# Attention, keys, values and gates: one more step between copies and the matmuls that read them, and matmuls of zeros at the start

## The chip, the core and the metric

The kernel runs on one core of a Trainium2 chip. The time is device microseconds of the whole program; three runs of the kernel before gave 1306.21, 1309.69 and 1312.1 us, median 1309.69. Names of engines: PE is TensorE (matmuls and transposes), DVE is VectorE, ACT is ScalarE, POOL is GpSimd, SP is SyncE, which issues the DMAs.

## The reference, cut to what matters

One layer of a hybrid decoder for 1024 prompt tokens and 32 sample tokens, in float32. An input projection of 22 column tiles feeds two groups of heads: four gated-delta heads (a chunked recurrence with a triangular inverse, decays from a gate) and eight heads of sliding-window attention with a learned sink. Then an output projection with a residual and a LayerNorm, a SwiGLU layer with a residual and a second LayerNorm. The parts that the change touches are the gate and the window attention:

```python
g = -jnp.exp(a_log) * jax.nn.softplus(a_a + dt_bias)        # gate: cumulated over a chunk
s = jnp.einsum('bnqhgd,bnkhd->bnhgqk', qb, kbk) * (HD_B ** -0.5)
s = jnp.where(mask, s, -jnp.inf)
p = jax.nn.softmax(jnp.concatenate([s, sink], axis=-1), axis=-1)[..., :KB]
o = jnp.einsum('bnhgqk,bnkhd->bnqhgd', p, vbk)
x = layernorm(ALPHA * x + m)                                 # ssum: the sum over D for the mean
```

## The kernel before, in words

All tokens are held with features on partitions. The tokens are cut in two halves, s = 0 (512 columns) and s = 1 (512 and the 32 sample columns, done as 272 + 272). Every float32 product is made of three matmuls on numbers split in a high and a low part (lines 426 to 428: high weight by high x, high weight by low x, low weight by high x). ACT writes the high part, DVE the low part (lines 161 and 162 for weights, 345 and 346 for x).

For each half `mix_in` runs through the projections one after the other (`dense`), and between two parts of a `dense` it calls `unit`, which lets the waiting pieces of attention, gates and recurrence take their next steps. Such a piece is a Python generator: it issues instructions, then yields the time that its PE work is worth; `pump` gives each generator one step at a call until a budget (2750, then 3000) is used up. A `yield 0.0` costs no budget, but what follows it is issued one `unit` later, so that more dense matmuls stand in front of it on PE. On top of that a scheduler places the issued instructions on each engine by its own estimate of the times, so the order on an engine is not that of the code alone. Each engine then runs its queue in order.

PSUM has eight banks: four for `dense` ("acc") and four for everything else ("ms"). SBUF pages come from pools ("hp", "xs", "xp"); taking a page issues a POOL memset of one column (line 228), which waits until the last user of that page is done. So POOL, too, has a queue in which a memset can stand in front of work.

The pieces that the change touches:
- `gating` (from line 480): transposes the gate inputs, a chain of some 25 short DVE and ACT operations, then matmuls at lines 537 to 541 that cumulate over time, a transpose at 555.
- `delta_k`: transposes at line 654 and products at 656 of the keys of the delta heads. `sample_attn`, `sample_delta`: the sample tokens; their updated states go out at line 1413 (`out_S_s`).
- `keys` and `vals`: split or transpose keys and values (lines 973, 995, 1002).
- `attn` (for each half four members m, each the heads m and m + 4, two members at a time): scores at lines 1059 and 1060, masking on DVE at 1063, exp on ACT at 1077, scaling on DVE at 1085; then for four tiles n the transposes at 1100, the copy from PSUM at 1104 (DVE for even n, ACT for odd n) and the product with the values at 1112.
- `out_proj` and `ln1`: DVE writes a residual tile `ac` (line 1681), POOL adds it up in `sum` (1683, 1685), PE takes the mean by a matmul with ones (1474).

Of the kernel before, what the change touches and what calls it, by code (L numbers as in the profile page):

```python
# [15 lines left out]
P = 128  # L16
# [77 lines left out]
NXP = 19  # L94
NRAW = 8
NSPLIT = 4
HLEAD = 5
HLAG = 3

# [108 lines left out]
def _program(k):  # L208
    nc, I, O = k.nc, k.I, k.O
    mm = nc.tensor.matmul  # L210
# [105 lines left out]
    def have(tag, n=1):  # L316
        while not room(tag, n):
            yield BLOCK
# [18 lines left out]
    def x_item(s, kt):  # L337
# [12 lines left out]

        return fin

    W.load(1)
    fins = [x_item(0, kt) for kt in range(3)]
    W.load(2)
# [128 lines left out]
    def gating(s, baT):  # L484
        w = 16 + s
        g = {}
        gt = small([P, 21, 17], "gt", 2)
        names = ["beta", "x", "ab", "y", "den", "y2", "pl", "gg", "gc", "gtot", "gd", "eg", "egl", "ekd", "bg", "ngc"]
        for i, n in enumerate(names):
            g[n] = gt[:, i, :]  # L490
        g["t"] = gt
        gba = gt[:, 16:18, :]
        pk = gt.rearrange("p a b -> p (a b)")[:, 18 * 17:18 * 17 + 32].rearrange("p (k w) -> p k w", w=16)
        gat[s] = g
        yield from have("ms")
        pt = bank()
        for n in range(4):
            tr(pt[:, n * 8:(n + 1) * 8], baT[:, n * P:(n + 1) * P], ident[:8, :8])
        if s:
            tr(pt[0:32, 32:40], baT[:, 512:544], ident[:8, :8])  # L500
        drop()
        V.tensor_copy(gba[:, :, 0:16].rearrange("p k (h n) -> p k h n", n=4),
                      pt[:, 0:32].rearrange("p (n k h) -> p k h n", k=2, h=4))
        if s:
            for h in range(4):
                V.tensor_copy(gba[32 * h:32 * h + 32, :, 16:17],
                              pt[0:32, 32:40].rearrange("p (k h) -> p k h", h=4)[:, :, h:h + 1])
        drop("ms")
        q = {n: g[n][:, :w] for n in names}
        A.activation(q["beta"], gba[:, 0, :w], AF.Exp, scale=-1.0)  # L510
        V.tensor_tensor(q["x"], gba[:, 1, :w], DT[:, :w], ALU.add)
        V.scalar_tensor_tensor(q["ab"], q["x"], -1.0, q["x"], ALU.mult, ALU.max)
        A.activation(q["y"], q["ab"], AF.Exp, scale=-1.0)
        yield 300.0
        V.tensor_scalar(q["beta"], q["beta"], 1.0, None, ALU.add)
        V.reciprocal(q["beta"], q["beta"])
        V.tensor_scalar(q["den"], q["y"], 2.0, None, ALU.add)
        V.reciprocal(q["den"], q["den"])
        V.tensor_tensor(q["y"], q["y"], q["den"], ALU.mult)
        V.tensor_tensor(q["y2"], q["y"], q["y"], ALU.mult)  # L520
        pl = q["pl"]
        V.tensor_scalar(pl, q["y2"], 1.0 / 13, 1.0 / 11, ALU.mult, ALU.add)
        for cf in (9, 7, 5, 3, 1):
            V.tensor_tensor(pl, pl, q["y2"], ALU.mult)
            V.tensor_scalar(pl, pl, 1.0 / cf, None, ALU.add)
        V.scalar_tensor_tensor(pl, pl, 2.0, q["y"], ALU.mult, ALU.mult)
        V.tensor_scalar(q["x"], q["x"], 0.0, None, ALU.max)
        V.tensor_tensor(pl, pl, q["x"], ALU.add)
        V.scalar_tensor_tensor(q["gg"], pl, -1.0, EA[:, :w], ALU.mult, ALU.mult)
        if s:  # L530
            yield from have("hp")
            su, so = late("SU", "SO")
        yield 0.0
        yield from have("ms")
        gg = g["gg"]
        pg = bank()
        mm(pg[:, 0:16], C["U"], gg[:, 0:16], start=True, stop=True)
        mm(pg[:, 17:33], C["ones"], gg[:, 0:16], start=True, stop=True)
        if s:
            mm(pg[:, 16:17], su, gg[:, 16:17], start=True, stop=True)  # L540
            mm(pg[:, 33:34], so, gg[:, 16:17], start=True, stop=True)
            drop()
        V.tensor_copy(gt[:, 8:10, :w], pg[:, 0:34].rearrange("p (k w) -> p k w", w=17)[:, :, :w])
        drop("ms")
        V.tensor_tensor(q["gd"], q["gtot"], q["gc"], ALU.subtract)
        A.activation(gt[:, 11:14, :w], gt[:, 8:11, :w], AF.Exp)
        V.tensor_tensor(q["bg"], q["beta"], q["eg"], ALU.mult)
        V.tensor_scalar(q["ngc"], q["gc"], -1.0, None, ALU.mult)
        V.tensor_copy(pk[:, 0, :], g["gc"][:, 0:16])
        V.tensor_copy(pk[:, 1, :], g["beta"][:, 0:16])  # L550
        yield 700.0
        yield from have("ms")
        yield from have("hp")
        pp = bank()
        tr(pp[:32, :P], pk.rearrange("p k w -> p (k w)"), ident)
        gT = page([32, P], F32, f"gT{s}")
        V.tensor_copy(gT, pp[:32, :P])
        drop("ms")
        gd = k.dp.tile([32, P], F32, name=f"gd{s}")
        dma(out=gd, in_=gT)  # L560
        drop()
        g["dram"] = gd
        flags.add(("g", s))
        yield 150.0
# [391 lines left out]
    def keys(s, kb):  # L956
        yield from have("hp", 4)
        kh = [page([P, 512], F32R, f"kh{s}{i}") for i in range(2)]
        kl = [page([P, 512], F32R, f"kl{s}{i}") for i in range(2)]
        for i in range(2):  # L960
            a, o = slice(64 * i, 64 * i + 64), slice(64 - 64 * i, 128 - 64 * i)
            A.copy(kh[i][a, :], kb[a, 0:512])
            A.copy(kh[i][o, :], kb[a, 0:512])
            V.tensor_tensor(kl[i][a, :], kb[a, 0:512], kh[i][a, :].bitcast(F32), ALU.subtract)
            V.tensor_tensor(kl[i][o, :], kb[a, 0:512], kh[i][a, :].bitcast(F32), ALU.subtract)
            yield 0.0
        at[s, "k"] = (kh, kl)
        if s:
            G.tensor_copy(ksT, kb[:, 512:544])
            yield from have("ms")  # L970
            yield from have("hp")
            pt = bank()
            tr(pt[:, 0:P], kb[:, 384:512], ident)
            tr(pt[0:32, P:2 * P], kb[:, 512:544], ident)
            kp = page([P, 2, P], F32, "kp")
            V.tensor_copy(kp[:, 0, :], pt[:, 0:P])
            V.tensor_copy(kp[0:32, 1, :], pt[0:32, P:2 * P])
            drop("ms")
            dma(out=O["k_p"], in_=kp[:, 0, :])
            dma(out=O["k_s"][:, 124:128, :], in_=kp[0:32, 1, :])  # L980
            drop()
            dma(out=O["k_s"][:, 0:124, :], in_=I["cache_k"][:, 4:128, :])
            dma(out=O["v_s"][:, 0:124, :], in_=I["cache_v"][:, 4:128, :])
        drop()
        flags.add(("keys", s))
        yield 300.0

    def vals(s, vT):
        yield from have("hp")
        vN = page([P, 4, P], F32, f"vN{s}")  # L990
        yield 0.0
        yield from have("ms")
        pv = bank()
        for n in range(4):
            tr(pv[:, n * P:(n + 1) * P], vT[:, n * P:(n + 1) * P], ident)
        V.tensor_copy(vN, pv.rearrange("p (n t) -> p n t", t=P))
        drop("ms")
        if s:
            dma(out=O["v_p"], in_=vN[:, 3, :])
            yield from have("ms")  # L1000
            pt = bank()
            tr(pt[0:32, 0:P], vT[:, 512:544], ident)
            V.tensor_copy(vnew[0:32, :], pt[0:32, 0:P])
            drop("ms")
            dma(out=O["v_s"][:, 124:128, :], in_=vnew[0:32, :])
        drop()
        at[s, "v"] = vN
        flags.add(("vals", s))
        yield 600.0
# [21 lines left out]
    def attn(s, m, qs):  # L1031
# [49 lines left out]
        for n in range(4):  # L1081
            w0 = P if (s == 0 and n == 0) else 0
            for i in range(2):
                t = sts[n][:, i, w0:]
                V.tensor_scalar(t, t, su[:, n, i:i + 1], None, ALU.mult)
            if n == 1:
                yield 0.0
        yield from have("ms", 2)
        yield from have("hp", 2)
        po = bank()  # L1090
        pts = {}
        for n in range(5):
            if n < 4:
                w0 = 1 if (s == 0 and n == 0) else 0
                yield from have("ms")
# [7 lines left out]
                for a, z in (((1, 2), (3, 4)) if w0 else ((0, 4),)):  # L1103
                    (A.copy if n % 2 else V.tensor_copy)(pts[n][:, a:z, :], pt[:, a:z, :])
                drop("ms")
            if n:
                c = n - 1
                w0 = 1 if (s == 0 and c == 0) else 0
                for b in range(w0, 2):
                    vb = vN[:, c, :] if b else (vN[:, c - 1, :] if c else vcar)  # L1110
                    for i in range(2):
                        mm(po[64 * i:64 * i + 64, c * P:(c + 1) * P], vb[:, 64 * i:64 * i + 64], pts[c][:, 2 * i + b, :],
                           start=(b == w0), stop=(b == 1), tile_position=(0, 64 * i))
                drop()
            yield 1000.0
        A.copy(mixed[s, 4 + m][:, 0:512], po)
        drop("ms")
        flags.add(("att", s, m))
# [962 lines left out]
```

## Time and profile before

| what | value |
|---|---|
| median of three runs | 1309.69 us |
| the profiled execution | 1308.84 us, span 1307.0 us |
| PE busy | 1249.6 us, 96% |
| DVE, ACT, POOL busy | 887.3, 620.2, 393.4 us |
| granted PE clock, mean | 0.986 |

The span runs from the first to the last instruction; 1.8 us of the execution lie outside it. PE is the engine to watch: where it is idle, or where its clock is below 1, the program gets longer. In the rows, "x4" after a row is the number of instructions merged, "[5.21 <-X]" is idle time of the engine before the row and what ended it. A float32 matmul shows as two records on PE.

### The profile page before, as it was taken

To read this page: it belongs to the slowest core of one execution; us is meant where nothing else is said; L and a number is where in the kernel's file an instruction comes from. 1 tells how busy PE (TensorE), PEld (TensorE's weight loads), DVE (VectorE), ACT (ScalarE), POOL (GpSimd) and SP (SyncE) were. 2 spreads that over 40 slices of the span, in tenths; PEclk is the share of its full clock that TensorE was granted. 3 is DMA by queue.
4 is the path that set the end of the run, shared out by engine and by line. 5 is a ranking of instruction groups with operands and counts; after the bars stand their busy time and mean duration, and the time that the engine had idled before them with its cause. 6 is when DMAs were issued, how large, how long until landed. Compare 5 with 4: busy or idle time off the path is not lost.

```text
span 1307.0 us, 25072 instructions
## 1 busy us (share of the span) xinstructions
PE 1249.6 (96%) x8673; PEld 1126.6 (86%) x8673; DVE 887.3 (68%) x2040; ACT 620.2 (47%) x1376; POOL 393.4 (30%) x1207
## 2 busy tenths in 40 slices
PE   8999899989899998997899999999999999999996
PEld 6877689988899987985899999999999999788995
DVE  6787975887986777868856665555555765632674
ACT  7765644656755542577322223223333554622453
POOL 1009410205713133436744332332321112111210
PEclk9999999999999998998899999999999999999998
DMA  7431341242223545545454432222323886643461
GB/s 256 130 89 66 89 134 46 87 127 65 62 83 125 170 142 163 180 135 192 143 156 140 142 108 75 90 70 78 104 91 101 279 284 187 201 121 108 142 220 47
DMA packets 119103, 170.82 MB, mean 131 GB/s; under 512 B 20272, under 2 KB 50096, under 8 KB 118960
## 3 DMA queue, kind: packets, MB, share of 16 engines
q1 hardware_dynamic: 118976, 169.22, 41.3%
q8 instruction: 68, 1.11, 0.3%
q14 instruction: 59, 0.48, 0.1%
HBM read 138.44 MB, written 31.75 MB: 130 GB/s over the span
## 4 chain that ended last, share of the span: by engine, by line
PE 79%; DVE 10%; ACT 3%; issue 3%; DMA 3%; POOL 2%; SPq 0%; DVEq 0%; ACTq 0%; POOLq 0%
PE acc L427 6%; PE acc L428 6%; PE acc L426 6%; PE acc L1796 6%; PE acc L1797 6%; PE acc L1798 6%; PE acc L1967 6%; PE acc L1965 6%; PE acc L1966 6%; PE ms L1798 5%; PE ms L1796 5%; PE ms L1797 5%; DMA hr<-hd 1%; DVE wl L162 1%; DVE st L1063 1%
## 5 line engine op out<-in xcount | busy, mean ns | idle before, releaser
L162 DVE TENSOR_TENSOR wl<-wr,wh 128x512 fp32r<-128x512 f32 x330 | 242.2, 737 | 143.5 <-ACT wh L161 137.4
L161 ACT CAST wh<-wr 128x512 fp32r<-128x512 f32 x330 | 197.5, 602 | 261.2 <-PE acc L1966 104.2
L426 PE MATMUL acc<-xh,wh 128*128 128x272 f32 (+1 forms) x528 | 174.9, 331 | 6.0 <-ACT xh L345 5.2
L427 PE MATMUL acc<-xl,wh 128*128 128x272 f32 (+1 forms) x528 | 174.0, 330 | 0.0
L1967 PE MATMUL acc<-hx,wl 128*128 128x272 f32 (+1 forms) x528 | 171.8, 326 | 2.0 <-DVE wl L162 2.0
L428 PE MATMUL acc<-xh,wl 128*128 128x272 f32 (+1 forms) x528 | 173.6, 329 | 0.0
L1965 PE MATMUL acc<-hx,wh 128*128 128x272 f32 (+1 forms) x528 | 172.5, 327 | 1.0 <-ACT wh L161 1.0
L161 ACT CAST wh<-S 128x512 fp32r<-128x512 f32 x88 | 54.4, 619 | 148.0 <-PE acc L1797 96.3
L426 PEld LDWEIGHTS acc<-xh,wh 128*128 128x128 f32 x528 | 100.8, 191 | 13.2 <-ACT xh L345 5.2
L1967 PEld LDWEIGHTS acc<-hx,wl 128*128 128x128 f32 x528 | 99.9, 189 | 11.3 <-DVE wl L162 3.3
L1965 PEld LDWEIGHTS acc<-hx,wh 128*128 128x128 f32 x528 | 99.8, 189 | 9.7 <-POOL hx L228 1.2
L427 PEld LDWEIGHTS acc<-xl,wh 128*128 128x128 f32 x528 | 100.6, 191 | 8.6 <-issue 1.8
L428 PEld LDWEIGHTS acc<-xh,wl 128*128 128x128 f32 x528 | 100.8, 191 | 7.0 <-issue 0.2
L1966 PE MATMUL acc<-hx,wh 128*128 128x272 f32 x352 | 101.9, 290 | 0.0
L162 DVE TENSOR_TENSOR wl<-S,wh 128x512 fp32r<-128x512 f32 x88 | 71.3, 812 | 37.4 <-ACT wh L161 34.7
L1966 PE MATMUL acc<-hy,wh 128*128 128x512 f32 x176 | 69.5, 395 | 0.0
L1966 PEld LDWEIGHTS acc<-hx,wh 128*128 128x128 f32 x352 | 67.0, 191 | 0.3
L428 PE MATMUL acc<-mh,wl 128*128 128x272 f32 (+1 forms) x192 | 63.4, 330 | 0.0
L426 PE MATMUL acc<-mh,wh 128*128 128x272 f32 (+1 forms) x192 | 62.9, 328 | 0.0
L427 PE MATMUL acc<-ml,wh 128*128 128x272 f32 (+1 forms) x192 | 62.5, 326 | 0.0
L1694 ACT CAST hx<-hr 128x272 fp32r<-128x272 f32 (+1 forms) x66 | 31.5, 486 | 52.3 <-DMA hr<-hd 49.8
L1798 PE MATMUL ms<-T2h,wl 128*128 128x272 f32 x176 | 50.8, 289 | 0.0
(629 smaller groups left out, 3481.8 us busy)
## 6 DMA issues: line engine op xcount, KB each, us to landing
wr<-in_w_ffo_t SPq DMA_DIRECT2D x120, 256.0 KB, 2.9
wr<-in_w_ffi_t SPq DMA_DIRECT2D x108, 256.0 KB, 2.8
wr<-in_w_in_t SPq DMA_DIRECT2D x88, 256.0 KB, 2.7
wr<-in_w_out_t SPq DMA_DIRECT2D x32, 256.0 KB, 2.9
hd<-x SPq DMA_DIRECT2D x22, 272.0 KB, 2.8
hr<-hd SPq DMA_DIRECT2D x44, 136.0 KB, 2.7
hd<-x SPq DMA_DIRECT2D x22, 256.0 KB, 2.0
hr<-hd SPq DMA_DIRECT2D x22, 256.0 KB, 4.8
```

Of the source, the lines that this page charges most:

```text
L161: nc.scalar.copy(hi, raw)
L162: nc.vector.tensor_tensor(lo, raw, hi.bitcast(F32), ALU.subtract)
L426: mm(ps[:, :cw], wh, xh[kt][:, c0:c0 + cw], start=(kt == 0), stop=False)
L427: mm(ps[:, :cw], wh, xl[kt][:, c0:c0 + cw], start=False, stop=False)
L428: mm(ps[:, :cw], wl, xh[kt][:, c0:c0 + cw], start=False, stop=(kt == n - 1))
L1694: A.copy(hi, raw)
L1796: mm(o, wh[:, kt, :], xh, start=(start and kt == 0), stop=False, **kw)
L1797: mm(o, wh[:, kt, :], xl, start=False, stop=False, **kw)
L1798: mm(o, wl[:, kt, :], xh, start=False, stop=(kt == 3), **kw)
L1965: mm(ps, wh[:, f % 4, :], xh, start=(f == 0), stop=False)
L1966: mm(ps, wh[:, f % 4, :], xl, start=False, stop=False)
L1967: mm(ps, wl[:, f % 4, :], xh, start=False, stop=(f == NF - 1))
```

## The change

Before the first DMA-fed work, a tile of zeros is made on DVE and 14 matmuls of 128 x 128 of it are issued to PE. In `gating`, `keys` (s = 1) and `vals` one more `yield 0.0` stands between a step that ends in a DVE or ACT write and the PE instructions that read it. In `attn` the scaling is cut after tiles 1 and 3, not after 1 alone; the loop over tiles has six turns, not five, so that the product with the values of tile c is issued two turns after its transposes, not one; and a turn is valued at 800, not 1000.

```diff
@@ -349,6 +350,12 @@
+    zero = cpt([P, 256], "zero")
+    V.memset(zero, 0.0)
+    warm = acc()
+    for _ in range(WARM):
+        mm(warm[:, 0:P], zero[:, 0:P], zero[:, P:256], start=True, stop=True)
@@ -530,6 +537,7 @@   (gating)
+        yield 0.0
         yield 0.0
         yield from have("ms")
@@ -967,6 +975,7 @@   (keys, s = 1)
             G.tensor_copy(ksT, kb[:, 512:544])
+            yield 0.0
             yield from have("ms")
@@ -989,6 +998,7 @@   (vals)
         yield 0.0
+        yield 0.0
         yield from have("ms")
@@ -997,6 +1007,7 @@   (vals, s = 1)
             dma(out=O["v_p"], in_=vN[:, 3, :])
+            yield 0.0
             yield from have("ms")
@@ -1083,13 +1094,13 @@   (attn)
-            if n == 1:
+            if n % 2:
                 yield 0.0
...
-        for n in range(5):
+        for n in range(6):
             if n < 4:
...
-            if n:
-                c = n - 1
+            if n > 1:
+                c = n - 2
...
-            yield 1000.0
+            yield 800.0
```

The instructions are the same but for the zeros; their order moves on every engine from the start to the first LayerNorm, and not after it. In the pieces below each kernel has its own line numbers: 1100, 1112 and 1685 of before are 1111, 1123 and 1696 of the change.

POOL, at the end of the output projection of the first half. `sum00` is the sum for the first LayerNorm, `ac7` its last term, `l10sq` and `xr12` are pages. Before:

```order
L228 MEMSET l10sq_6998 128x1
...
L228 MEMSET l10sq_7003 128x1
...
L228 MEMSET l10sq_7043 128x1
L228 MEMSET xr12_7047 128x1
L1685 TENSOR_TENSOR sum00_6075<-sum00_6075,ac7_6780 128x512
L228 MEMSET l10sq_7084 128x1
```

The same place in the change:

```order
L229 MEMSET l10sq_6974 128x1
...
L1696 TENSOR_TENSOR sum00_6035<-sum00_6035,ac7_6773 128x512
L229 MEMSET l10sq_7015 128x1
...
L229 MEMSET l10sq_7020 128x1
...
L229 MEMSET l10sq_7060 128x1
L229 MEMSET xr12_7064 128x1
```

The last addition stood behind four page memsets of that stretch; it now stands in front of them, behind the memset of `l10sq_6974`, whose counterpart before stands in front of it as well.

PE, second half, third attention member (s = 1, m = 2), tile 0: `st120` is its scaled scores, `ptS120` the transposed copy. Before:

```order
L1100 MATMUL ms_4613<-cst_72,st120_4285 128x128 x2
...
L1100 MATMUL ms_4695<-cst_72,st121_4287 128x128 x4
...
L428 MATMUL acc_4751<-xh1_5_2624,wl73_4603 128x272
L1112 MATMUL ms_4612<-ptS120_4618,vcar_188 64x128 x2
L1112 MATMUL ms_4612<-ptS120_4618,vN1_3447 64x128 x2
```

The same in the change:

```order
L1111 MATMUL ms_4935<-cst_72,st120_4484 128x128 x4
...
L1111 MATMUL ms_5053<-cst_72,st121_4486 128x128 x4
...
L1111 MATMUL ms_5118<-cst_72,st122_4488 128x128 x4
L1123 MATMUL ms_4934<-ptS120_4940,vcar_205 64x128 x2
L1123 MATMUL ms_4934<-ptS120_4940,vN1_3453 64x128 x2
L1123 MATMUL ms_4934<-ptS121_5058,vN1_3453 64x128 x4
```

Between transposes and reader stood 25 rows of PE's queue after the last of them; now 135 rows stand there, among them the transposes of two more tiles.

PE in the change, second half, tiles 2 and 3 of member 0 and tiles 0 to 2 of member 1:

```order
L1111 MATMUL ms_4115<-cst_72,st110_3692 128x128 x2
L1111 MATMUL ms_4170<-cst_72,st102_3599 128x128 x3
L1123 MATMUL ms_4045<-ptS100_4051,vcar_205 64x128 x2
...
L1111 MATMUL ms_4182<-cst_72,st111_3694 128x128 x4
...
L1111 MATMUL ms_4239<-cst_72,st103_3601 128x128 x4
L1111 MATMUL ms_4251<-cst_72,st112_3696 128x128 x4
```

Here transposes of two tiles follow each other, each in a bank of its own ("ms_" with its number), while two more banks hold the running products of the two members.

## Rows read from the trace of the kernel before

**Rows 1.** Page, part 1: busy time, share of the span, instructions.

```profile
PE 1249.6 (96%) x8673; PEld 1126.6 (86%) x8673; DVE 887.3 (68%) x2040; ACT 620.2 (47%) x1376; POOL 393.4 (30%) x1207
```

**Rows 2.** Windows: stretch and its length, busy time by engine, granted clock, DMA.

```profile
60.00:160.00 100.00, 90.93 (x558) 72.16 (x557) 88.49 (x282) 62.65 (x176) 44.85 (x110) 1.00 0.27 81
...
240.00:360.00 120.00, 108.69 (x865) 102.78 (x864) 102.64 (x344) 80.16 (x238) 51.17 (x126) 0.97 0.32 91
500.00:520.00 20.00, 14.79 (x96) 13.37 (x95) 10.73 (x21) 5.64 (x10) 8.51 (x51) 0.83 0.53 164
```

**Rows 3.** Waits of PE: who waited for whom, total us, times, longest.

```profile
PE ms L1112 <- DVE ptS L1104: 5.8, 5, 1.9
PE ms L1474 <- POOL l10sq L228: 5.2, 1, 5.2
...
PE ms L1100 <- ACT junk L798: 3.0, 2, 2.5
PE ms L1059 <- DVE ast L1063: 2.6, 4, 1.4
PE ms L1100 <- DVE st L1085: 2.4, 3, 1.6
PE ms L537 <- DVE gt L529: 2.0, 1, 2.0
...
PE ms L973 <- ACT junk L660: 1.0, 1, 1.0
```

**Rows 4.** Windows of 2 us behind three of these waits.

```profile
258.00:260.00 2.00, 2.00 (x15) 2.00 (x14) 0.37 (x4) 1.76 (x2) 0.00 (x0) 0.68 0.80 253
260.00:262.00 2.00, 2.00 (x10) 2.00 (x10) 0.33 (x2) 1.89 (x11) 0.10 (x1) 0.50 0.74 267
320.00:322.00 2.00, 2.00 (x16) 1.67 (x17) 0.00 (x0) 0.20 (x1) 1.87 (x5) 0.54 0.40 119
322.00:324.00 2.00, 2.00 (x12) 2.00 (x12) 0.00 (x0) 0.00 (x0) 1.81 (x3) 0.60 0.00 0
510.00:512.00 2.00, 1.09 (x3) 0.57 (x3) 0.00 (x0) 0.00 (x0) 0.89 (x2) 0.50 0.62 190
512.00:514.00 2.00, 2.00 (x8) 1.48 (x7) 0.98 (x2) 0.21 (x1) 0.10 (x1) 0.50 0.58 211
```

**Rows 5.** Timeline at the first LayerNorm: start us, us, what, idle before.

```profile
501.83 0.68 DVE L1681 SCALAR_TENSOR_TENSOR ac<-xr,acc 128x512 f32<-128x512 f32 x1
...
503.65 2.42 SPq L1413 DMA_DIRECT2D out_S_s<-S  x4
...
507.00 0.10 POOL L228 MEMSET l10sq<- 128x1 f32 x1 [3.00 <-DMA out_S_s<-S]
...
509.60 1.26 POOL L1685 TENSOR_TENSOR sum<-sum,ac 128x512 f32<-128x512 f32 x1
...
510.91 1.22 PE L1474 MATMUL ms<-sum,ones_r 128*128 128x512 f32 x1 [5.21 <-POOL l10sq L228]
```

**Rows 6.** Timeline of the start.

```profile
5.18 0.80 PE L426 MATMUL acc<-xh,wh 128*128 128x512 f32 x1 [5.18 <-ACT xh L345]
...
9.12 0.60 PE L428 MATMUL acc<-xh,wl 128*128 128x512 f32 x1
...
9.54 0.41 PE L426 MATMUL acc<-xh,wh 128*128 128x512 f32 x1
...
9.66 2.77 DVE L346 TENSOR_TENSOR xl<-xraw,xh 128x512 fp32r<-128x512 f32 x4 [0.22 <-ACT xh L345]
...
12.71 0.40 PE L427 MATMUL acc<-xl,wh 128*128 128x512 f32 x1
12.94 0.40 PE L428 MATMUL acc<-xh,wl 128*128 128x512 f32 x1
```

**Rows 7.** Chain that ended last: start us, us, what.

```profile
41.32 0.89 PE ms L656 x8
...
308.12 0.68 DVE ptS L1104
```

More of the change, by code (lines that the diff above doesn't have):

```diff
@@ L96 @@
 NSPLIT = 4
+WARM = 14
 HLEAD = 5
```

## The prediction

> **What bounds the kernel now.** I read the busy shares first: PE is busy 96% of the span, every other engine 68% or less [rows 1]. So the time is PE's own work plus the time in which PE stands still or runs at a lower clock. The windows tell where that is: from 60 to 160 us PE is idle 100 - 90.9 = 9.1 us, from 240 to 360 another 11.3 us, from 500 to 520 another 5.2 us [rows 2]. The first two stretches are attention, gates, keys and values of the two halves; the last is the first LayerNorm. Then the waits of PE give each loss a name [rows 3]: the product with the values waits for the copy of the transposed scores (5.8 us in five waits), transposes wait for the bank that a delta head's squares still read (3.0), or for the scaling (2.4), the scores wait for a bank (2.6), the gate's matmuls for DVE (2.0), the LayerNorm's mean for POOL (5.2).
>
> Behind three of those waits the granted clock falls to 0.50, which is 1.2 of 2.4 GHz [rows 4]. What that costs is busy time times the missing share: 258 to 262 us 2.0 x 0.32 + 2.0 x 0.50 = 1.6 us, 320 to 324 us 2.0 x 0.46 + 2.0 x 0.40 = 1.7 us, 510 to 514 us 1.09 x 0.50 + 2.0 x 0.50 = 1.5 us. In each case PE had been idle for about 2 us or more just before (2.0, 1.9 and 5.2, the longest waits of their lines in rows 3).
>
> **The LayerNorm at 510 us.** This is the largest single wait, and the diff does not name it. DVE has written the last term at 502.5 (501.83 + 0.68). POOL adds it only at 509.60, since its queue holds memsets of pages in front, and these wait for the stores of the sample states, issued at 503.65; the first memset is released at 507.00 after 3.00 us [rows 5]. PE waits 5.21 us. In the changed order of POOL the addition stands in front of the memsets that wait for the second four stores. Those in front of it wait for the earlier stores, or for what is long done. So the addition can start once its term is there, and takes 1.26 us. PE's matmul moves ten 272-column matmuls later in its own queue, 1.3 us, so it finds the sum ready: the second group of state updates on PE stands some 4 us later than before, which delays DVE and the term, but 53 rows of PE still stand between that group and the mean, worth 7 to 8 us, and the chain of eight updates (about 2.2 us), the term (0.68) and the addition (1.26) is some 4 to 5. I take away the wait and the slow clock behind it: 5.2 + 1.5 = 6.7 us. Bounds: 0, if a late store of the first group still stands in front of it, and 6.7.
>
> **Attention, gates, keys, values.** I counted how much PE work stands between each wait's source and the waiting instruction, in both orders, at the row durations. Of the five waits of the product with the values (5.8 us in sum), four get more distance than they waited (the place with st120 goes from 25 rows behind its transposes to 135), and the longest, 1.9, gets 1.3 more: 5.2 us go. The gate's matmuls in the second half stand 4 us further from their transposes than before, against a wait of 2.0: gone. The two transposes that wait for a bank held by squares stand 14 and 17 us later against scores of their own: 3.0 go. Of the waits for scaling (2.4) two small ones go, 0.8 in sum; the large one keeps its distance. The wait at the key outputs (1.0) keeps its own, too. Together 5.2 + 2.0 + 3.0 + 0.8 = 11.0 us.
>
> That is before what comes back. The same DVE work is done in the same stretch (88.5 of 100 us busy and 102.6 of 120, [rows 2]), so a copy can be as late as before wherever DVE's queue is long. New tight places show: in the changed order transposes of two tiles follow each other with only two free banks, the inverse's second step in the second half stands 3.3 us behind its first, not 6.2. What the new waits cost the trace of before can't show; bounds are 0 and the whole 11.0. I take 5.0, nearer the middle. The falls of the clock at 258 and 320 hang on waits that go (2.0 and 1.9), worth 3.3; I take half, 1.7, since a new wait of 2 us would bring one back. Net 11.0 - 5.0 + 1.7 = 7.7 us.
>
> **The zeros at the start.** A float32 matmul of 128 x 128 is two records; eight records took 0.89 us [rows 7], so one is 0.22 us, and 14 are 3.1 us at 2.4 GHz or 6.2 at 1.2. PE is idle until 5.18 us. From 5.18 to 9.54 the first nine matmuls of 512 columns start 0.43 us apart, which is 1.2 GHz (the column of the granted clock does not show it); the last ones of the block, from 12.71 on, 0.23 apart [rows 6]. If the zeros start near 1.1 us they end between 4.2 and 7.3, so the first block may begin up to 2.1 us later, but runs at 0.23 a matmul: 24 of them take 5.6 us, from 7.3 to 12.9. The block can't end earlier than that in any case: DVE splits the last four x tiles one after the other until 12.43 (9.66 + 2.77), and two matmuls follow the last, 0.46 us. Its last matmul starts at 12.94 now and would start at about 12.7 [rows 6]. I take 0.25 us; if the zeros do not help the clock, the delay of up to 2.1 us is the loss; the gain can't be over 0.3.
>
> The Trainium skill (TensorE: Matmul & The Clock Gate, Part 1) says that a cold PE needs time under load, not a number of matmuls, before it runs at the full clock. By that the zeros would take the slow phase off the first block, nine matmuls by 0.20 us, 1.8 us instead of 0.25, and the sum would be 1.5 us lower. The rows agree with the rule that the start is slow, but the splits on DVE set the end of the block, so I do not use it.
>
> **Sum.** 1308.84 (the profiled execution) - 6.7 - 7.7 - 0.25 = 1294.2 us. The median of the runs is 0.85 us above the profiled one, so 1295 us. The extra turn of the loops adds no instruction: the PE work of before and of the change is the same but for the zeros, and from the first LayerNorm's end on the order is the same, so everything later stays.
>
> **Rivals.** First, the waits in attention only move: the new waits eat all of the 11.0 and bring the falls of the clock back, and only the LayerNorm and the start are left: 1309.7 - 6.7 - 0.25 = 1302.7. For it speaks DVE's load; against it that the waits were a few long ones, 1 to 2.5 us, with DVE free in between. Second, the LayerNorm's wait stays, since the state updates come later on PE: 1309.7 - 7.7 - 0.25 = 1301.7. For it, 1 to 3 us of slack is little; against it, the memsets that it waited for no longer stand in front. Third, slower: the bank. Each member's running product holds a bank, so two members leave two for transposes, and with two tiles in flight a transpose must wait until a copy has emptied one. A copy is 0.68 us [rows 7]. There are 32 such tiles (eight members, four tiles). The gains gross are 6.7 + 11.0 + 3.3 + 0.25 = 21.3, so it turns slower from 21.3 / 32 = 0.67 us a tile on, about a whole copy in every one; at 0.9 us a tile, a copy that waits for other DVE work, it is 1309.7 + 28.8 - 21.3 = 1317. For it, the bank waits of the scores (2.6 in four, [rows 3]); against it, most tiles have 5 to 8 us of other PE work on either side. Fourth, nothing changes: both the LayerNorm's wait and the others come back in other places, 1309.
>
> **How the numbers follow.** Forecast 0.52, first rival 0.18, second 0.12, third 0.08, fourth 0.10. What can be told from no change is 0.5%, 6.5 us, so faster means under 1303.1 us. The forecast lies under it, as do some half of the first rival and two thirds of the second: 0.52 + 0.09 + 0.08, and a little of the fourth, 0.71. Slower means over 1316.2: part of the third, 0.06. The rest, 0.23, is the same. The forecast's own range is 1287 (no new waits, 1309.7 - 22, rounded) to 1302; with the second and fourth rivals the range that holds 8 in 10 is 1287 to 1308.
>
> **What would show it.** In the profile after: PE's wait before the mean's matmul (one 5.2 us row) is gone or under 1 us, and the granted clock of the 20 us around it is 1.00, not 0.83; idle PE time of the two attention stretches falls from 20.4 us to about 14 or less; waits of the product for the copy fall from 5.8 us to under 2; the gate's wait of 2.0 is gone; the last matmul of the first block starts at about 12.7 us. The prediction is wrong if the idle time of the attention stretches stays near 20 us, or if bank waits (transposes or scores waiting for a copy or for the masking) take its place.

## The result and the profile after

The changed kernel took 1297.92 us (median of 5 runs, 1295.16 to 1304.28), the kernel before in the same rounds 1307.64 (5 runs, 1303.08 to 1312.1): a ratio of 0.9929 [0.9909, 0.9949], 9.7 us less. The forecast of 1295 us lies 2.9 us below. The profiled execution took 1296.37 us, its span is 1294.6, 12.4 us shorter than the span before.

Page, part 1, of the changed kernel: PE's busy time is nearly what it was in [rows 1] (4.1 us more, with 6.1 us of zeros in it), in a shorter span.

```profile
PE 1253.7 (97%) x8701; PEld 1130.8 (87%) x8701; DVE 889.3 (69%) x2041; ACT 619.0 (48%) x1376; POOL 396.1 (31%) x1207
```

The windows of the changed kernel (columns as in [rows 2]):

```profile
60.00:160.00 100.00, 94.08 (x563) 75.40 (x562) 87.92 (x296) 64.96 (x184) 44.33 (x106) 0.97 0.28 82
240.00:360.00 120.00, 114.04 (x915) 110.02 (x914) 106.33 (x346) 79.94 (x251) 50.94 (x122) 0.97 0.30 88
360.00:500.00 140.00, 137.21 (x1316) 122.07 (x1315) 104.65 (x284) 66.44 (x158) 38.92 (x179) 0.99 0.48 142
500.00:520.00 20.00, 20.00 (x152) 19.04 (x151) 17.28 (x28) 8.36 (x14) 12.12 (x45) 1.00 0.75 234
```

PE is idle 5.9 us in the first stretch (9.1 before), 6.0 in the second (11.3), none at the LayerNorm (5.2), and 2.8 from 360 to 500 us, where it had been 1.2 (138.84 of 140 busy). PE's waits of the changed kernel, longest in total first:

```profile
PE ms L1070 <- DVE ast L1074: 5.0, 3, 4.2
...
PE ms L1070 <- DVE hs L415: 1.7, 1, 1.7
PE ms L982 <- ACT junk L668: 1.7, 1, 1.7
...
PE ms L1417 <- DVE S L1422: 1.2, 2, 0.9
...
PE ms L563 <- ACT gt L554: 1.0, 1, 1.0
```

Against [rows 3]: the product with the values (now L1123), the mean (now L1485) and the gate's cumulation (now L545) have no row any more; a later row of the gate (L563) waits 1.0. New in its size is a single wait of 4.2 us of the scores (L1070) for a bank that DVE's masking (L1074) still reads; before, the longest of that kind was 1.4. The timeline of the changed kernel at the first LayerNorm, which answers to [rows 5]:

```profile
499.05 2.44 SPq L1424 DMA_DIRECT2D out_S_s<-S  x4
499.71 0.68 DVE L1692 SCALAR_TENSOR_TENSOR ac<-xr,acc 128x512 f32<-128x512 f32 x1
...
500.53 1.61 POOL L1696 TENSOR_TENSOR sum<-sum,ac 128x512 f32<-128x512 f32 x1 [0.23 <-DVE ac L1692]
...
502.74 1.02 PE L1485 MATMUL ms<-sum,ones_r 128*128 128x512 f32 x2
502.79 0.10 POOL L229 MEMSET l10sq<- 128x1 f32 x1 [0.41 <-DMA out_S_s<-S]
```

POOL adds the last term 0.23 us after it has nothing else to do, right behind DVE; the memset that waits for the second group of stores (502.79) comes after the addition, not before. PE finds the sum ready.

The start of the changed kernel, against [rows 6]:

```profile
1.18 6.11 PE L358 MATMUL acc<-zero 128*128 128x128 f32 x28 [1.18 <-DVE zero L355]
...
7.04 0.48 PE L433 MATMUL acc<-xh,wh 128*128 128x512 f32 x1
...
7.36 0.40 PE L434 MATMUL acc<-xl,wh 128*128 128x512 f32 x1
...
7.59 0.39 PE L435 MATMUL acc<-xh,wl 128*128 128x512 f32 x1
...
10.40 2.04 DVE L347 TENSOR_TENSOR xl<-xraw,xh 128x512 fp32r<-128x512 f32 x3 [0.22 <-ACT xh L346]
...
12.95 0.39 PE L435 MATMUL acc<-xh,wl 128*128 128x512 f32 x1
```

The zeros hold PE until about 7.0 us; the block starts 1.86 us later than before and then runs at about 0.23 us a matmul from its second on, but for two longer steps (0.43 us before 9.64 and 0.36 before 11.24, right behind splits that end at 9.49 and 11.10). DVE's last split ends at 12.44 (10.40 + 2.04), and the block's last matmul starts at 12.95 us (12.94 before). And three places where the clock is low, which answer to [rows 4]:

```profile
126.00:128.00 2.00, 2.00 (x7) 1.61 (x7) 2.00 (x9) 0.00 (x0) 1.80 (x5) 0.50 0.00 0
128.00:130.00 2.00, 2.00 (x7) 1.49 (x6) 2.00 (x12) 0.09 (x1) 1.84 (x3) 0.55 0.00 0
332.00:334.00 2.00, 2.00 (x11) 2.00 (x11) 1.90 (x7) 0.00 (x0) 1.84 (x3) 0.50 0.00 0
334.00:336.00 2.00, 2.00 (x11) 2.00 (x11) 2.00 (x7) 0.00 (x0) 1.79 (x3) 0.50 0.18 38
336.00:338.00 2.00, 2.00 (x11) 2.00 (x11) 2.00 (x9) 0.00 (x0) 1.89 (x5) 0.50 0.41 127
...
494.00:496.00 2.00, 2.00 (x12) 1.71 (x10) 2.00 (x6) 0.62 (x1) 0.32 (x6) 0.75 1.01 288
496.00:498.00 2.00, 2.00 (x10) 2.00 (x10) 2.00 (x8) 0.00 (x0) 0.29 (x8) 0.50 0.95 281
498.00:500.00 2.00, 2.00 (x17) 2.00 (x16) 2.00 (x8) 0.00 (x0) 0.37 (x10) 0.89 0.59 162
```

Before there were three such places too. By busy time times missing share, as in the prediction, they cost 4.8 us before; now 1.9 (126 to 130), 3.0 (332 to 338) and 1.7 (494 to 500), 6.6 us. With the edges of these stretches counted in on both sides it is 5.3 us before (windows at 262 and 514) and 7.2 now (windows at 124 and 330). So the waits went, and in this pair of executions the low clock did not.

### The profile page after: what moved, and what is told of

It reads as the page before. It is cut to its first block, busy times and chain, and to the rows that moved or that the text cites. A ratio compares the mean times of both kernels' runs of the same rounds, so it can differ in the third digit from the quotient of the medians.

```text
span 1294.6 us, 25112 instructions
## 1 busy us (share of the span) xinstructions
PE 1253.7 (97%) x8701; PEld 1130.8 (87%) x8701; DVE 889.3 (69%) x2041; ACT 619.0 (48%) x1376; POOL 396.1 (31%) x1207
## 4 chain that ended last, share of the span: by engine, by line
PE 77%; DVE 12%; issue 3%; ACT 3%; DMA 2%; POOL 2%; DVEq 0%; SPq 0%; ACTq 0%; POOLq 0%
PE acc L1978 6%; PE acc L1807 6%; PE acc L1976 6%; PE acc L1977 6%; PE acc L1808 6%; PE acc L1809 6%; PE acc L433 5%; PE acc L434 5%; PE ms L1809 5%; PE ms L1807 5%; PE acc L435 5%; PE ms L1808 5%; DVE wl L163 2%; DVE st L1074 1%; PE ms L1123 1%
## 5 line engine op out<-in xcount | busy, mean ns | idle before, releaser
L163 DVE TENSOR_TENSOR wl<-wr,wh 128x512 fp32r<-128x512 f32 x330 | 238.6, 726 | 133.6 <-ACT wh L162 123.5
L1647 POOL TENSOR_TENSOR S<-wr,S 128x512 f32<-128x512 f32 x22 | 34.7, 1577 | 54.5 <-DVE wl L163 54.5
```

Source lines behind the costliest of these rows:

```text
L163: nc.vector.tensor_tensor(lo, raw, hi.bitcast(F32), ALU.subtract)
L1647: G.tensor_tensor(t["S2"], W.get(r["A12"]), t["S2"], ALU.subtract)
```

## The experiments

Theory: the gain is the sum of two things, the order on POOL at the LayerNorm and the distance between copies and products. Rivals: one of the two is all of it; the gain is eaten by new waits; the zeros matter.

| run | what it is | median us | ratio to before [95%] |
|---|---|---|---|
| e1 | zeros alone | 1306.2 | 0.9994 [0.9978, 1.001] |
| e2 | attention part alone | 1298.82 | 0.9942 [0.9921, 0.9963] |
| e3 | extra steps in gate, keys, values alone | 1311.29 | 1.0034 [1.0018, 1.0051] |
| e4 | before without the memsets at the LayerNorm | 1301.91 | 0.9961 [0.9948, 0.9974] |
| e5 | attention: the loop alone | 1300.42 | 0.994 [0.992, 0.9959] |
| e6 | attention: the scaling's cut alone | 1296.75 | 0.9915 [0.9895, 0.9935] |
| e7 | e2 without the memsets at the LayerNorm | 1300.02 | 0.9938 [0.9916, 0.996] |
| e8 | the change without the zeros | 1296.51 | 0.9924 [0.9894, 0.9954] |
| e9 | the change without the memsets of `pre` | 1301.6 | 0.9935 [0.992, 0.995] |
| e10 | e8 without any page memset | 1331.29 | 1.0171 [1.0148, 1.0194] |
| e11 | e6 without any page memset | 1332.66 | 1.017 [1.015, 1.0191] |
| e12 | e6 with the extra steps in keys and values | 1301.93 | 0.9938 [0.9916, 0.996] |

Each ratio is against the kernel before on the same chip in the same rounds (medians 1307.13 for e1 to e4, 1308.53 for e5 to e8, 1309.94 for e9 to e11, 1308.28 for e12).

**The parts, e1 to e3.** In e1 the first hunk of the change alone, in e2 the `attn` hunks, in e3 the four `yield 0.0` of `gating`, `keys` and `vals`.

> The kernel before with the 14 matmuls of zeros alone; nothing else of the change. Its order on POOL and PE is that of before but for a few rows. Theory (the DVE splits set the end of the first block): within 0.5 us of before, the last matmul of the first block starts between 12.7 and 13.0 us, the LayerNorm's wait of 5.2 us on PE stays. Rival (the slow clock of the first block is what costs): about 1.8 us less, the block's last matmul at about 11.1 us.

> The kernel before with the attention part alone (six turns, a turn valued at 800, the scaling cut after tiles 1 and 3), no zeros, no extra steps in gates, keys and values. In its order POOL adds the last term in front of the memsets, as in the change. Theory (the LayerNorm's wait and the copies' waits are apart and add up): the LayerNorm's wait is gone, the product's wait for the copy falls from 5.8 to under 1 us, the gate's wait of 2.0 stays: 8 to 10 us less than before. Rival (the gain comes from the extra steps in gates, keys and values): under 4 us less.

> The kernel before with the extra steps in gates, keys and values alone. In its order, too, POOL adds the last term in front of the memsets. Theory: the gate's wait of 2.0 us and the LayerNorm's wait of 5.2 us go, the product's waits for the copy (5.8) stay: 5 to 8 us less than before. Rival (the product's waits are the price, the LayerNorm's is made good later): under 2 us less.

The zeros alone can't be told from nothing. Two of the expectations for e1 failed all the same. The LayerNorm's wait is 2.7 us, not 5.2, in the order of before; and the first block's last matmul starts later than before, not between 12.7 and 13.0:

```profile
9.55 3.44 DVE L347 TENSOR_TENSOR xl<-xraw,xh 128x512 fp32r<-128x512 f32 x5
...
13.49 0.39 PE L435 MATMUL acc<-xh,wl 128*128 128x512 f32 x1
```

The attention part alone gives 8.3 us (1307.13 - 1298.82). The extra steps alone make it slower, by 4.4 us [2.4, 6.7] by the ratio, which I had not expected: in e3 the addition does stand in front of the memsets that hold it up in [rows 5], but POOL is held by others, which wait for the first four stores. POOL, stores and the mean in e3:

```profile
503.62 2.92 SPq L1417 DMA_DIRECT2D out_S_s<-S  x4
...
506.69 0.10 POOL L228 MEMSET sum<- 128x1 f32 x1 [3.36 <-DMA out_S_s<-S]
...
507.63 0.10 POOL L228 MEMSET xr<- 128x1 f32 x1 [0.84 <-DMA out_S_s<-S]
508.52 0.10 POOL L228 MEMSET l10var<- 128x1 f32 x1 [0.79 <-DMA out_S_s<-S]
509.96 0.10 POOL L228 MEMSET l10var<- 128x1 f32 x1 [1.34 <-DMA out_S_s<-S]
510.02 1.26 POOL L1689 TENSOR_TENSOR sum<-sum,ac 128x512 f32<-128x512 f32 x1
510.73 0.69 DVE L1685 SCALAR_TENSOR_TENSOR ac<-xr,acc 128x512 f32<-128x512 f32 x1 [2.04 <-DMA xr<-in_xT]
...
512.88 2.08 PE L1478 MATMUL ms<-sum,ones_r 128*128 128x512 f32 x2 [3.92 <-POOL l10sq L228]
```

The addition before the last one waits behind four memsets (3.36 + 0.84 + 0.79 + 1.34), the last term waits for an `xr` page whose memset is one of them, and PE waits 3.92 us. This is the case of the lower bound that the prediction gave the LayerNorm's term ("if a late store of the first group still stands in front of it"). It tells why the gain did not come, not why e3 is slower: 3.9 is less than 5.2, and PE's idle time from 60 to 500 us is less too (19.2 us, 21.5 before). That stays open. The three parts sum to -0.9 - 8.3 + 4.2 = -5.0 us (against 1307.13); together they gave -9.7. They do not add.

**The LayerNorm by itself, e4.** PE's, DVE's and ACT's order are those of before; POOL has no memsets for the pages `l10sq` and `l10var`.

```diff
     def page(shape, dt, name, tag="hp"):
+        clear = not name.startswith(("l10sq", "l10var"))
...
-        G.memset(t[:, 0:1].bitcast(F32), 0.0)
+        if clear:
+            G.memset(t[:, 0:1].bitcast(F32), 0.0)
```

> The kernel before, with the one-column memsets of the LayerNorm's square and variance pages left out (line 228, pages l10sq and l10var of the first half); the order of PE and DVE is that of before word for word, the values are the same. Theory (PE waits at 510 us since POOL's addition stands behind memsets that wait for the stores): PE's wait falls from 5.2 to under 1 us and the clock behind it stays at 1.00, 6 to 7 us less than before, and the two attention stretches keep their 20 us of idle time. Rival (the squares need the stored pages anyway, so the wait only moves to ACT and to the variance's matmul): under 2 us less.

PE's wait before the mean is gone, and by the ratio 5.1 us [3.4, 6.8] with it, under the 6 to 7 expected. So the memsets in POOL's queue were the cause of [rows 5], and the term is worth about 5.

e4 also shows what a single execution can't tell. Near 151 us the same transposes, in the same order, wait 2.45 us in before and 2.36 in e4. The window behind that wait, in before and then in e4:

```profile
152.00:154.00 2.00, 2.00 (x10) 1.62 (x10) 1.94 (x6) 1.41 (x4) 0.08 (x1) 1.00 0.30 101
```

```profile
152.00:154.00 2.00, 2.00 (x6) 1.46 (x6) 1.94 (x6) 1.02 (x6) 0.28 (x2) 0.50 0.44 156
```

In before the clock stays at 1.00; in e4 it is low from 150 to 158 us and costs 3.1 us. From 60 to 546 us the low clock costs 11.3 us in e4's profiled execution (5.3 in before's), and PE's idle time from 60 to 500 us is 19.0 (21.5), though PE, DVE and ACT have the same order there. So a term that is read from one execution of each kernel is uncertain by some us.

**Attention cut in two, e5 and e6.** e5 has the six turns, `c = n - 2` and 800; e6 has only `if n % 2` in place of `if n == 1`.

> Of the attention part only the loop over tiles (six turns of 800, the product two turns after its transposes); the scaling is cut after tile 1 alone, as before. Theory: the product no longer waits for its copy (5.7 us in before, under 1 here), but the last addition of the LayerNorm's sum stands behind two page memsets again, and even the addition of the term before it behind three, so PE's wait at the mean stays at 3 to 6 us: about 1307 - 5 = 1302 us. Rival (bank): with two tiles in flight new waits for banks eat the gain: 1307 or more. Rival (order does not matter, only the distance): the whole gain of the attention part comes back, 1299 us.

> Of the attention part only the scaling's cut (after tiles 1 and 3); the loop over tiles as before (five turns of 1000, the product one turn after its transposes). Theory: the last addition of the LayerNorm's sum stands in front of the memsets, so PE's wait at the mean is under 1.5 us and 5 to 6.7 us go, while the product's waits for its copy stay at 4 to 6 us: about 1302 us. Rival (the earlier stores hold POOL all the same, as in the run with the extra steps alone): the wait stays at 3 to 4 us, 1306 to 1309. Rival (all of the gain lies in the loop): 1307.

Waits of PE in e5, and then in e6, for the product and the mean:

```profile
PE ms L1112 <- DVE ptS L1104: 3.1, 3, 1.6
...
PE ms L1474 <- POOL xr L228: 2.9, 1, 2.9
```

```profile
PE ms L1112 <- DVE ptS L1104: 2.3, 2, 1.4
...
PE ms L1112 <- ACT ptS L1104: 0.7, 1, 0.7
...
PE ms L1474 <- POOL l10sq L228: 0.3, 1, 0.3
```

In e5 the last addition stands behind two `l10sq` memsets, in e6 in front of them, and PE's wait at the mean is 2.9 and 0.3 us: with 5.2 in before, 2.7 in e1 (order of before), 0.8 in e2 and none in the change (addition in front), the place in POOL's order decides whether the wait is long or short, e3 apart. The other half of my expectation failed: e5's product still waits 3.1 us, e6's only 3.0, though the cut was not meant for it, and the one line of e6 gives as much as the whole change. By its time e5 (8.1 us below before) is the rival "the whole gain of the attention part comes back"; by distance alone, as that rival has it, it is not, since its product still waits. None of e6's rivals was right. Each edit shifts the order of everything behind it, and either gives most of the gain. PE's idle time shows where: from 60 to 500 us it is 15.7 us in e5 and 15.8 in e6, against 21.5 before, 19.0 in e2 and 14.8 in the change. So each half alone takes about the same idle time out of attention as the whole change does, and e6 the wait at the mean as well.

**Do the two add, e7; are the zeros worth anything, e8.** e7 is e2 with the edit of e4; e8 is the change without the zeros.

> The attention part alone, and no page memsets for l10sq and l10var, so that POOL's queue in front of the LayerNorm's sum holds none that waits for a store. Theory: the attention part has already taken that wait down to 0.8 us, so 0 to 1.5 us more: 1297.5 to 1299 us, the fastest of all by a little. Rival (the two are independent, the memsets alone gave 5.2): 1307 - 8.3 - 5.2 = 1293.6 us.

> The change without the zeros and their matmuls. Theory: DVE's splits set the end of the first block, zeros are worth nothing within 1 us either way: 1297 to 1299 us (the change 1297.9), and the last matmul of the first block starts at 12.9 us as with them. Rival (the zeros heat the clock up for the first block): 1.8 us slower than the change, 1299.7. Rival (the zeros only delay): 1 us faster, 1297. It also tells whether the attention part and the extra steps add (1298.8 and +4 would be 1303) or the extra steps cost nothing once the attention part is there (1298 to 1299).

e7 is no faster than e2, so the LayerNorm's gain is the same gain in both, as expected. e8 is 1.4 us below the change, within what can be told: the extra steps cost nothing once the attention part is there, and the zeros give nothing. In e8's profile the last matmul of the first block starts at 13.42 us, so the zeros gain that block 0.5 us against that execution, and nothing against the profile of before (12.94); e1, with zeros, has 13.49.

e7 and e2 show something else: PE, DVE and ACT have the same order in both. Windows of e2, then of e7, behind the same two short waits (0.91 and 0.55 us, at 495 to 497 us in both):

```profile
496.00:500.00 4.00, 3.45 (x29) 3.00 (x29) 4.00 (x13) 0.62 (x1) 0.33 (x6) 1.00 0.74 213
```

```profile
496.00:500.00 4.00, 3.45 (x20) 2.87 (x20) 4.00 (x13) 0.44 (x1) 0.53 (x12) 0.62 0.80 230
498.00:504.00 6.00, 6.00 (x25) 5.49 (x25) 6.00 (x20) 0.62 (x1) 1.07 (x24) 0.51 0.82 238
```

With as much busy time, 29 matmuls ran in the one and 20 in the other: at 2.4 GHz there, from about 497 us on at 1.2 here, and 6.0 x 0.49 = 2.9 us are lost from 498 to 504. The waits in front of it and PE's order alone do not decide it. The Trainium skill (TensorE: Matmul & The Clock Gate, Part 1) says that the number of slow matmuls at a kernel's start differs between runs of one kernel. The starts here agree (nine slow matmuls of the first block in before's execution, twelve in e8's, neither with zeros), and e2 and e7 show the like in the middle of a kernel.

**The new wait of 4.2 us, e9.** DVE and POOL of the changed kernel just before it:

```profile
118.44 0.25 DVE L410 TENSOR_SCALAR hs<-hs 128x4 int32<-128x4 int32 x1
...
120.97 0.64 POOL L710 TENSOR_TENSOR itmp<-Db,Ab 64x256 f32<-64x256 f32 x1
...
121.55 0.09 POOL L229 MEMSET pre<- 128x1 f32 x1
...
121.69 0.16 DVE L411 TENSOR_SCALAR hs<-hs 128x4 int32<-128x4 int32 x1 [3.00 <-issue]
121.71 0.06 DVE L624 MEMSET pre<- 128x3 f32 x1
...
125.12 0.58 PE L1070 MATMUL ms<-kh,qs 128*128 128x256 f32 x1 [4.21 <-DVE ast L1074]
```

The profile names nobody for DVE's 3.00 us ("issue"). The order does: in DVE's queue the memset of `pre` (L624) stands in front of L411 (the trace has their starts 0.02 us apart, the other way round) and waits for POOL's page memset, which ends at 121.64 behind a row of products for the triangular inverse. DVE starts 0.05 us later, and the scores' bank is freed that much later. e9 takes that page memset away, as in e4, for names that begin with `pre`; PE's order stays but for two rows.

> The change without the one-column page memset on POOL for the conv inputs (pre); PE's order as in the change but for two rows. In the change's profile the scores wait 4.2 us for a bank at 125 us; DVE, which empties that bank, stands still for 3.0 us until 121.69, and POOL ends the memset of a pre page at 121.64, behind its chain of products for the triangular inverse. Theory (the late bank is a page memset in POOL's queue, as at the LayerNorm): DVE's 3.0 us are gone, the scores' 4.2 us fall to under 1.5 and the low clock behind them (1.7 us) goes or moves: 1293 to 1296 us. Rival (the two members' running products hold the banks, POOL is a bystander): the 4.2 us stay and the time is the change's, 1297 to 1299.

The wait fell as expected; DVE has no idle time there, and PE in e9 shows

```profile
118.78 0.06 DVE L626 MEMSET pre<- 128x3 f32 x1
...
122.46 0.39 PE L1072 MATMUL ms<-kh,qs 128*128 128x256 f32 x1 [1.25 <-DVE ast L1076]
```

So POOL was the cause, not the two members' products in their banks; what is left, 1.25 us, is near the longest such wait of before, 1.4. Yet the time is no better, 0.9935 against 0.9929. In e9 DVE's order differs in some rows, and one of them brings a wait of the same size 240 us later:

```profile
360.15 2.87 SPq L725 DMA_DIRECT2D Eall<-ed  x4
...
363.42 0.70 DVE L732 STREAM_TRANSPOSE Dl<-Eall 32x512 f32<-32x512 f32 x1 [3.65 <-DMA Eall<-ed]
...
364.17 0.31 PE L740 MATMUL ms<-Dl,Ball 32*32 32x32 f32 x2 [4.11 <-DVE hs L412]
```

A transpose that waits for a DMA now stands one row earlier in DVE's queue, in front of a short operation that PE needs. The granted clock from 360 to 374 us is 0.51 in e9, another 4.8 us (9.89 busy x 0.49).

**No page memsets, e10 and e11; a last combination, e12.** In e10 and e11 the line `G.memset(t[:, 0:1].bitcast(F32), 0.0)` is gone; e12 adds the extra steps of `keys` and `vals` to e6.

> The change without the zeros at the start and without any of the one-column page memsets on POOL; the order moves on every engine. Theory (memsets in POOL's queue cost the change some 3 to 5 us, the zeros nothing): 1290 to 1295 us, the fastest so far. Rival (a new order brings other waits of the same size): 1296 to 1300.

> Only the scaling's cut after tiles 1 and 3, on the kernel before, and none of the one-column page memsets on POOL; the order moves on every engine. With the memsets this cut alone took 1296.75 us, with 3.0 us of waits of the product for its copy and a 3.3 us wait at the values that they do not explain. Theory (memsets cost waits wherever POOL is busy): 1292 to 1295 us. Rival (the LayerNorm's memsets were the only ones that counted in this order, and their wait was already 0.3 us): 1296 to 1298.

> On the kernel before: the scaling's cut after tiles 1 and 3, and the extra steps in keys and values, not the one in the gate (with it and the old loop the last addition of the LayerNorm's sum falls back behind two page memsets), no zeros, the old loop. The cut alone took 1296.75 us and had a wait of 3.3 us at the second half's values, which the extra step in vals is meant to take. Theory (the waits that a trace shows add up): 1293 to 1295 us, the fastest, with the LayerNorm's wait under 1 us. Rival (a wait that is taken away comes back elsewhere, as with the conv inputs' memsets): 1296 to 1300 us. Against the change (1297.92 us, ratio 0.9929) a ratio under 0.9905 would count as a win.

e10 and e11 are a miss of 36 to 41 us: without the memsets the order moves on every engine, and PE waits longer for ACT (in e10 13.5 us in four waits of L1800, 5.0 in two in the change). Which of the moved rows does it was not taken further; what e4 and e9 show of single memsets does not hold for all of them together. e12 did not beat e6: the wait at the values that it was meant to take (3.3 us in e6) is there again, 3.2 us. No version beats the change by more than can be told; e6, one line, equals it.

## Why the prediction came out right, and which terms did not

- **The LayerNorm's wait (5.2 us).** Right in size and cause. The wait is gone because the addition stands in front of the memsets, and e4, with the memsets gone and nothing else moved on PE, gives 5.1 us. The risk named with it was real: in e3 the first stores hold POOL.
- **Attention, gates, keys, values (idle time).** Forecast 11.0 gross, 5.0 back, 6.0 net. From 60 to 500 us PE's idle time fell from 21.5 (9.07 + 11.31 + 1.16) to 14.8 us (5.92 + 0.16 + 5.96 + 2.79), 6.7 net; in the two stretches to 11.9, where "about 14 or less" was forecast. That the size came out is in part luck: the 5.0 was picked between two bounds, and e4 has 19.0 with the order of before. The waits of the product and of the gate's cumulation went, as worked out from the distances; but that the distances make the net gain is not shown, since e5 and e6 have 15.7 and 15.8 with about 3 us of the product's waits left. That new waits would come was right; that banks of the running products would make the largest was not: it was POOL's queue (e9).
- **The clock.** This is the step that failed. The prediction took away 1.5 us at the LayerNorm and half of 3.3 in attention, 3.2 us in all. The low clock at 510 went (1.00 from 500 to 520 us), that at 258 and 320 went, but others came at 124, 331 and 494, and the sum went from 5.3 to 7.2 us: 5.1 us off. That the change itself makes more low clock is not shown: e4 has 11.3 us in the order of before, and the mean granted clock is 0.986 over the change's five runs and over 25 runs of before (0.982 to 0.991). "A new wait of 2 us would bring one back" was too narrow a rule: the fall at 494 came behind no wait over 0.9 us, e2 and e7 had or had not a fall behind the same waits, and the prediction passed over the wait of 2.45 us near 151 us in before, with no fall behind it.
- **The zeros (0.25 us).** Worth nothing in the time (e1, e8). The mechanism was as told: about 0.23 us a matmul from the second on, and the splits on DVE set the end of the block. The size was not. In before, in the change and in e1 the block's last matmul starts 0.50 to 0.51 us behind the end of the last split (12.44, 12.44 and 12.99); the prediction had room for one matmul there, 0.23 (12.43 to about 12.7), and the rest, 0.27, is all of the 0.25 that it booked. By the rule of the Trainium skill (TensorE: Matmul & The Clock Gate, Part 1) the time of the slow phase would have come back, 1.8 us by the prediction's rows: the slow phase is gone, as the rule has it, but the time went into the zeros.
- **The sum.** 5.2 + 6.0 + 3.2 + 0.25 = 14.65 was forecast; 5.2 + 6.7 - 1.9 + 0 = 10.0 is what the same terms measure in the profiled pair. That pair differs by 12.4: some 0.95 of the rest lie behind 546 us, where the order is the same, and about 1.5 are in gaps that no row here names. The medians differ by 9.7, two thirds of the forecast gain. That the forecast time, 1295, is only 2.9 us off is in part luck: it started from 1309.69, and before had a median of 1307.64 in the rounds of the result, 2.05 us less.

The rival "the LayerNorm's wait stays" is e3's case, "slower by banks" was not seen: e5 and e2, with two tiles in flight, are faster than before. What no run settles is why either half of the attention part alone is worth nearly all of it; the runs show where the idle time goes, and that the gains do not add.

## What to carry to other kernels

A step that only moves instructions is worth what the waits in its new order cost, and that is read from the queue in front of each waiting instruction: look above all for housekeeping (page memsets, waits for stores) that stands in front of the one operation that the busiest engine needs. A trace names the waits of its own order; the gains of two edits need not add, so test each combination as its own kernel. Put a saving of clock behind a shorter wait into the range, not into the forecast, and compare several executions before a term of a few us is read from one.

## What had not been expected of the hardware

With PE, DVE and ACT in the same order and the same two waits (0.91 and 0.55 us), one execution went on at 2.4 GHz and the other at 1.2 GHz for some 6 us, worth 2.9 us. Near 151 us before and e4 differ in the same way, behind 2.45 and 2.36 us at the same place of the same order, worth 3.1 us. Single runs of one kernel lie up to 9 us apart (the change: 1295.16 to 1304.28), so a fall or two of the clock is as large as many of the edits here.
